# A hybrid pooling and gated-attention block on one core: the score recursion placed between the products of the projection pairs, and the pooling branch placed in front

## The chip, the cores and the metric

The kernel runs on one core of a Trainium2 chip. The metric is device time in microseconds for one execution of the whole block. The kernel before takes 1304.01 us, the median of three runs (1301.28 to 1304.34). The five engines of the core are written PE (matrix products), DVE (elementwise with two inputs), ACT (functions and copies), POOL (a second, slower elementwise engine) and SP (which issues the DMAs).

## The reference, cut to what matters

One encoder block on 1024 tokens of width 1024, with 16 meta tokens in front, in float32:

```python
z = u @ w_in;  a, q, k, v, r, lr, ga, gb = split(z)
p = multiscale_pool(a)                  # trailing means over 2, 4, 8, 16 tokens, minus the token
p = (p grouped @ w_pool_mix) * pool_scale;  y_a = p @ w_pool_out
log_a = log_sigmoid(lr @ w_gate_up + b_gate) / 16
# per chunk of 64 tokens and per head (4 heads, dk 64, dv 128):
b = cumsum(log_a);  scores = sum_k q_t k_s exp(-|b_t - b_s|)
o = scores @ v + (q exp(b)) @ S;  S = exp(b_end) S + (k exp(b_end - b))^T v
o = rmsnorm(o) * silu(r);  y_b = o @ w_gla_out
m = sigmoid(ga) * y_a + sigmoid(gb) * y_b
h = h + m @ w_out;  h = h + relu(rmsnorm(h) @ w_ff1)^2 @ w_ff2;  out = rmsnorm(h)
```

## The kernel before, in words

Every large product is made of three PE products of 128x128 weights with 512 columns (or 264): each float32 operand is split into a high part (rounded by ACT) and a low part (the difference, on DVE or POOL), and high x high, high x low and low x high are added (`mm3`). The order of the PE's work is the order in which the code is written. The other engines' instructions stand in an order that a scheduler makes from the dependences, and each engine then works its own queue in order.

The stages, in order of the program:

1. `start`: norm, transposition and the projections to v and to the low-rank decay input.
2. `proj_open` and `k_block`: differences of the transposed input for the next stage, and the projection to k (two blocks of 128 columns).
3. `pairs_of_projections`: the projections to q, r, gb and ga, eleven pairs of 128-column blocks. Each pair takes seven products (a Strassen scheme: P1 to P7) of 12 matmuls, 77 products in all. `sums_weights` makes the sums of weights that a product needs (four per pair, on DVE), and `split` parts them (ACT, then DVE), three products ahead, in four slots. After each product DVE combines sums of banks (`u2`, `u3`, `c`), and `put_...` finishes an output: for a gate ACT takes Abs, Exp and Ln, DVE one operation (`sigmoid`), ACT one more Exp, and a DMA stores it in HBM.
4. `gla`, the attention stage. The matmuls of `fill` run between the steps of the attention: the four blocks of `a_block` (the projection to the pooled columns), `mix_block` (pooling sums on DVE and 24 matmuls), the 16 blocks of `ya_block`, and the `yb_block`s of the first half of the tokens. A unit is a pair of heads p with a half of the tokens, four in all. `inside` computes the scores of a unit by a recursion of six levels: per level two multiplications on DVE (`grow`), a copy on ACT, 32 small matmuls (`scores`) and one predicated copy on DVE into `scc`. `across` then does what needs the state: transposition of k, eight chained state updates on DVE, the products with v and with the state, the norm, and the second transposition. Each unit's `inside` runs beside the `across` of the unit before it. `pour` drives the filling work by written costs: each step yields a cost, and as much filling work follows, times `PACE`.
5. The second half of `yb_block`, the output product (`out_tile`), and the two feed-forward products.

Buffers of the stages lie over one another: the left and right stacks are popped at each stage's opening. PSUM has eight banks; in the pairs stage four (`y`), two (`z`) and two (`sc`).

Of the kernel before, what the change touches and what calls it, by code (L numbers as in the profile page):

```python
# [31 lines left out]
PACE, LEVEL, OPENING = 1.0, 1.6, 10.0  # L32
# [71 lines left out]
def kernel(  # L104
# [34 lines left out]
    def two(tag):  # L139

        if tag == "sc":
            if "sc" not in wide:
                wide["sc"] = psp["sc"].tile([P, 2, 512], F32, name="b_sc", tag="sc")
            return wide["sc"]
        return psp[tag].tile([P, 2, 512], F32, name=f"b_{tag}", tag=tag)
# [7 lines left out]
    q_dram = dp.tile([2, 2, P, HALF], F32, name="q_dram")  # L153
    v_dram = dp.tile([2, 8, P, 2 * P], F32, name="v_dram")
# [6 lines left out]
    small = left.push("small", [P, 160], F32)  # L161
    small_at = [0]

    def tiny(n):
        a = small_at[0]
        small_at[0] += n
        assert small_at[0] <= 160
        return small[:, a : a + n]
# [6 lines left out]
    metab = left.push("metab", [P, 4, 16], F32)  # L175
    lrT_meta = left.push("lrT_meta", [16, 32], F32)[:, :META]
# [9 lines left out]
    MH, ML = [], []  # L186
# [185 lines left out]

    base = left.mark()
# [62 lines left out]
    def proj_open():  # L436

        left.pop_to(base)
        right.pop_to(1)
        S["t"] = [tuple(left.push(f"t{i}{k}", [P, 4, HALF], F32R) for k in "hl") for i in range(4)]  # L440
        buffer("t1", 2)
        buffer("o", 3)
        piece = lambda half, j: S["xr"][:, 4 * j : 4 * j + 4, half * HALF : (half + 1) * HALF]
        b11, b21, b12, b22 = (piece(h, j) for h in range(2) for j in range(2))

        def parts(i, a, eng=dve):
            hi, lo = S["t"][i]
            act.activation(hi, a, ACT.Copy)
            eng.tensor_tensor(lo, a, f32(hi), ALU.subtract)

        dve.tensor_tensor(b11, b12, b11, ALU.subtract)
        parts(0, b11)
        pool.tensor_tensor(b12, b22, b12, ALU.subtract)
        dve.tensor_tensor(b22, b22, b11, ALU.subtract)
        parts(1, b22)
        dve.tensor_tensor(b21, b21, b22, ALU.subtract)
        parts(2, b12, pool)
        parts(3, b21)

    step(one, proj_open)  # L460

    def k_block(p):
        def evac(b, half, at, n):
            o = nxt("o")[:, :n]
            act.activation(o, b, ACT.Copy)
            c = at if half == 0 else META + HALF
            nc.sync.dma_start(k_dram[p, :, c : c + n], o)

        return lambda wb: project(wb, WITH_META, evac)

    for p in range(2):
        step(one, k_block(p), W1, [w_cols(C_K + p * P)])
# [10 lines left out]
    def put_q(d, half, b):  # L483
        o = nxt("o")
# [3 lines left out]
    def put_r(h, half, b):  # L488
        t, o = sigmoid(b), nxt("o")
# [4 lines left out]
    def put_gate(dram):  # L494
        def put(d, half, b):
            t, o = sigmoid(b), nxt("o")
            act.activation(o, t, ACT.Exp)
            nc.sync.dma_start(dram[d, half], o)

        return put  # L500
# [48 lines left out]
    def sums_weights(n_pairs, load):  # L549

        for p, i in sums_order(n_pairs):
# [3 lines left out]
            else:  # L555
                a21, a22 = (w1raw[i, 1][:, k : k + 4] for k in (0, 4))
                s = quad(S["fs"][:, i % 2] if p != "P7" else S["s3"])
                if p == "P5":
                    dve.tensor_tensor(s, a21, a22, ALU.add)
                elif p == "P6":  # L560
                    dve.tensor_tensor(s, s, a11, ALU.subtract)
                elif p == "P7":
                    dve.tensor_tensor(s, a11, a21, ALU.subtract)
                elif p == "P3":
                    dve.tensor_tensor(s, a12, s, ALU.subtract)
# [11 lines left out]
    def pairs_of_projections():  # L577
# [10 lines left out]
        buffer("c", 3, HALF, right)  # L588
        load(1, 0)
        load(1, 1)  # L590
        banks(keep=1, y=4, z=2)
        w1_slots()
        plain = lambda half, j: tuple(t[half][:, 4 * j : 4 * j + 4, OFF[half] : OFF[half] + HALF] for t in (TH, TL))
        x = {"P1": plain(0, 0), "P2": plain(0, 1), "P5": S["t"][0], "P3": plain(1, 1)}
        x.update(zip(("P6", "P7", "P4"), S["t"][1:]))
        xb, zb = {}, {}
        left_over = 7 * len(PAIRS)
        W1.shift = 1
        for p, i, (ah, al) in ahead(sums_weights(len(PAIRS), load), 3):
# [9 lines left out]
            left_over -= 1  # L609
            if left_over == 2:  # L610
                raw.back()
                enqueue(rest)
                W1.top_up(1)
# [4 lines left out]
            elif p == "P2":  # L618
                put(d, 0, xb.pop(i))
            elif p == "P6":  # L620
                dve.tensor_tensor(u2, b, u2, ALU.add)
            elif p == "P7":
# [3 lines left out]
                put(d + 1, 1, c)  # L626
            elif p == "P4":
                c = nxt("c")
                dve.tensor_tensor(c, b, u3, ALU.add)
                put(d + 1, 0, c)  # L630
            elif p == "P3":
                c = nxt("c")
                dve.tensor_tensor(c, zb.pop(i), u2, ALU.add)
                put(d, 1, c)
            yield

# [3 lines left out]

    def told(name):
        step(fill, lambda: done.add(name))

    def gla_open():
        W1.eng = pool
        left.pop_to(base)
        right.pop_to(0)
        S["yg"] = {1: right.push("yg1", [P, 2, HEADS, HALF], F32R)}
        S["kq"] = [right.push(f"kq{h}", [P, 2, 2, HALF + OFF[h]], F32) for h in range(2)]
        S["v"] = right.push("v", [P, 2, 4, 2 * P], F32)  # L650
        for p in range(2):
            for h in range(2):
                c = slice(META + HALF, None) if h else slice(0, META + HALF)
                nc.sync.dma_start(S["kq"][h][:, p, 0], k_dram[p, :, c])
                nc.sync.dma_start(S["kq"][h][:, p, 1, OFF[h] :], q_dram[p, h])
        load_v(0)
        buffer("t1", 3, HALF, right)
        buffer("o", 3, HALF, right)
        push = right.push
        S["N"] = [push(f"n{i}", [P, HALF, 2], F32) for i in range(2)]  # L660
        S["F"] = push("f", [P, HALF, 2], F32)
        S["yt"] = push("yt", [P, 2, HALF], F32)
        S["ends"] = push("ends", [P, HALF], F32)
        S["scc"] = push("scc", [P, 2, 2, 4, CH], F32)
        S["S"] = push("S", [P, 2, 2, P], F32)
        S["W"] = push("W", [P, NC - 1, P], F32)

        mix = push("mix", [P, 4, HALF], F32)
        S["kt"], S["qe"], S["kl"], S["g"] = quad(mix[:, 0]), mix[:, 1], mix[:, 2], mix[:, 3]
        S["on"], S["sr"] = mix[:, 0:2].rearrange("p a (b c) -> p (a b) c", b=4), mix[:, 2:4]  # L670
        S["right_gla"] = right.mark()
        buffer("a", 4, 1056, right)
        banks(keep=1, mm=3, m2=1, ms=1)

    def load_v(half):
        for p in range(2):
            nc.sync.dma_start(S["v"][:, p], v_dram[p, 4 * half : 4 * half + 4].rearrange("t p c -> p t c"))

    step(rest, gla_open)

    pooled = {}

    def a_block(g):
        def fn(wb):
            a = pooled[g] = nxt("a")

            def evac(b, half, at, n):
                c = at if half == 0 else META + HALF
                act.activation(a[:, c : c + n], b, ACT.Copy)

            yield from project(wb, WITH_META, evac)

        return fn

    def pool_open():
        left.pop_to(left_ff)
        S["pm"] = left.push("pm", [P, 2, 4, SEQ], F32R)
        S["ph"] = left.push("ph", [P, 2, SEQ], F32R)
        buffer("s", 2, 1056)
        mw = S["mw"] = left.push("mw", [P, 2, 4, P], F32R)  # L700
# [113 lines left out]
    for g in range(4):  # L814
        step(fill, mix_block(g))
# [632 lines left out]
```

## Time and profile before

| | before |
|---|---|
| time, median of three | 1304.01 us |
| time of the profiled execution | 1304.01 us |
| its span, first to last instruction | 1302.2 us |
| granted PE clock, mean of the span | 0.975 |
| PE busy | 1225.4 us (94%) |
| DVE busy | 881.4 us (68%) |
| ACT busy | 635.2 us (49%) |
| POOL busy | 77.4 us (6%) |

The profiled execution's own time is 1.8 us more than its span, and it is the median of the runs. In the profile, L and a number is a line of the kernel; a row of a group gives the engine, the line, the written tile and the read tiles with their shapes, how often it ran, busy time and mean duration, and the idle time of the engine ahead of it with what ended that. A row of the timeline gives the start and the duration in us. A row of the stage table gives a stretch from A to B, its length, and the busy time of PE, its weight load, DVE, ACT and POOL in it, then the granted share of the PE clock, the DMA engines' share and GB/s.

### The profile page before, as it was taken

The page shows a single profiled execution, that of the slowest core. Times are in us where ns is not written, and L with a number is a line of the kernel's source. Part 1 is how long each engine was busy: PE and PEld are TensorE (multiplying, and loading weights), DVE is VectorE, ACT ScalarE, POOL GpSimd, SP SyncE. Part 2 cuts the span into 40 slices and gives each one's busy share as a digit, 9 for nine tenths or more (in the row PEclk, how much of TensorE's full clock was granted, in tenths as well). Part 3 has the DMA queues.
Part 4 walks back from the last instruction along what each step waited for, and adds up shares of the span by engine and source line. Part 5 has one row for each costly group of instructions (what it writes and reads, how often), then busy time and mean ns, then how long its engine had stood idle before and what let it go on. Part 6 is the DMA issues. An engine that isn't in the chain of part 4 may idle for free.

```text
span 1302.2 us, 18212 instructions
## 1 busy us (share of the span) xinstructions
PE 1225.4 (94%) x6763; PEld 1005.7 (77%) x6763; DVE 881.4 (68%) x1433; ACT 635.2 (49%) x1115; POOL 77.4 (6%) x42
## 2 busy tenths in 40 slices
PE   5999999999993989699999999999999999999997
PEld 4997888888772767588878888888887788888776
DVE  4563776676569668573588676767665777887686
ACT  6643576777443333231465455455454444444544
POOL 2120000000111013340000000000000000000000
PEclk9999999999995989799999999999999999999999
DMA  7322343423510456482125444354459873333532
GB/s 233 104 57 74 99 120 97 128 83 113 180 42 32 138 170 187 163 290 65 81 81 162 146 162 154 134 167 153 157 177 350 293 260 105 98 91 96 162 90 89
DMA packets 149721, 181.74 MB, mean 140 GB/s; under 512 B 11488, under 2 KB 88560, under 8 KB 149632
## 3 DMA queue, kind: packets, MB, share of 16 engines
q1 hardware_dynamic: 149632, 180.58, 43.1%
q8 instruction: 53, 0.87, 0.3%
q14 instruction: 36, 0.29, 0.1%
HBM read 123.90 MB, written 56.64 MB: 139 GB/s over the span
## 4 chain that ended last, share of the span: by engine, by line
PE 77%; DVE 8%; ACT 2%; issue 2%; DMA 2%; SPq 0%; POOL 0%; ACTq 0%; DVEq 0%; POOLq 0%
PE b_o L257 7%; PE b_o L258 7%; PE b_o L256 7%; PE b_y L256 6%; PE b_y L257 6%; PE b_y L258 6%; PE b_mm L256 5%; PE b_mm L257 5%; PE b_mm L258 5%; PE b_z L257 4%; PE b_z L258 4%; PE b_z L256 4%; PE b_sc L256 3%; PE b_sc L257 3%; PE b_sc L258 3%
## 5 line engine op out<-in xcount | busy, mean ns | idle before, releaser
L525 ACT ACTIVATE w1h<-raw 128x512 fp32r<-128x512 f32 x106 | 65.9, 623 | 54.4 <-PE b_y L257 17.3
L526 DVE TENSOR_TENSOR w1l<-raw,w1h 128x512 fp32r<-128x512 f32 x106 | 72.7, 686 | 23.8 <-ACT w1h L525 23.8
L525 ACT ACTIVATE w1h<-fs 128x512 fp32r<-128x512 f32 x81 | 51.2, 632 | 63.9 <-PE b_y L257 39.8
L256 PE MATMUL b_o<-w1h 128*128 128x512 f32 x192 | 75.4, 393 | 2.7 <-DVE h L1274 1.7
L257 PE MATMUL b_o<-w1l,w1h 128*128 128x512 f32 x192 | 74.9, 390 | 1.3 <-DVE w1l L526 1.3
L258 PE MATMUL b_o<-w1h,w1l 128*128 128x512 f32 x192 | 75.3, 392 | 0.1
L526 DVE TENSOR_TENSOR w1l<-fs,w1h 128x512 fp32r<-128x512 f32 x81 | 55.6, 687 | 24.7 <-ACT w1h L525 24.7
L76 POOL TENSOR_TENSOR w1l<-raw,w1h 128x1024 fp32r<-128x1024 f32 x14 | 35.1, 2508 | 405.0 <-ACT w1h L75 405.0
L1322 DVE TENSOR_TENSOR bt<-w,w 128x512 f32<-128x512 f32 x80 | 54.8, 685 | 3.1 <-DMA w<-in_w_ff_dram 3.1
L525 ACT ACTIVATE w1h<-bt 128x512 fp32r<-128x512 f32 x45 | 28.4, 632 | 58.1 <-issue 33.8
L257 PE MATMUL b_o<-fxl,fxh 128*128 128x512 f32 x128 | 50.3, 393 | 0.6 <-DVE small L215 0.6
L256 PE MATMUL b_sc<-mh,w1h 128*128 128x512 f32 x128 | 50.1, 392 | 0.8 <-ACT u2p L1246 0.8
L256 PE MATMUL b_mm<-wo,mh 128*128 128x512 f32 x128 | 50.7, 396 | 0.0
L257 PE MATMUL b_z<-ml,w1h 128*128 128x512 f32 x128 | 49.9, 390 | 0.4 <-DVE ml L1134 0.4
L258 PE MATMUL b_mm<-wo,ml 128*128 128x512 f32 x128 | 50.2, 392 | 0.0
L257 PE MATMUL b_mm<-wo,mh 128*128 128x512 f32 x128 | 50.2, 392 | 0.0
L258 PE MATMUL b_o<-fxh,fxl 128*128 128x512 f32 x128 | 50.2, 392 | 0.0
L257 PE MATMUL b_sc<-ml,w1h 128*128 128x512 f32 x128 | 50.0, 391 | 0.0
L256 PE MATMUL b_o<-fxh 128*128 128x512 f32 x128 | 49.9, 390 | 0.0
L258 PE MATMUL b_sc<-mh,w1l 128*128 128x512 f32 x128 | 49.8, 389 | 0.0
L258 PE MATMUL b_z<-mh,w1l 128*128 128x512 f32 x128 | 49.8, 389 | 0.0
L256 PE MATMUL b_z<-mh,w1h 128*128 128x512 f32 x128 | 49.8, 389 | 0.0
(353 smaller groups left out, 3663.6 us busy)
## 6 DMA issues: line engine op xcount, KB each, us to landing
hf_dram<-h SPq DMA_DIRECT2D x112, 256.0 KB, 2.0
raw<-hf_dram SPq DMA_DIRECT2D x112, 256.0 KB, 2.7
w<-in_w_ff_dram SPq DMA_DIRECT2D x64, 256.0 KB, 4.7
raw<-in_w_in_dram SPq DMA_DIRECT2D x22, 512.0 KB, 4.5
raw<-in_w_ff_dram SPq DMA_DIRECT2D x16, 512.0 KB, 4.2
rawx<-in_w_ff_dram SPq DMA_DIRECT2D x16, 512.0 KB, 4.3
rawp<-in_w_in_dram SPq DMA_DIRECT2D x10, 512.0 KB, 4.4
xs<-in_x_dram SPq DMA_DIRECT2D x8, 512.0 KB, 5.2
```

Of the source, the lines that this page charges most:

```text
L76: self.eng.tensor_tensor(lo, raw, hi.bitcast(F32), ALU.subtract)
L256: pe.matmul(ps, ah, bh, start=first and i == 0, stop=False, skip_group_check=more)
L257: pe.matmul(ps, ah, bl, start=False, stop=False, skip_group_check=more)
L258: pe.matmul(ps, al, bh, start=False, stop=last and i == n - 1, skip_group_check=more)
L525: act.activation(hi, a, ACT.Copy)
L526: dve.tensor_tensor(lo, a, f32(hi), ALU.subtract)
L1322: dve.tensor_tensor(bt, w, S["w2"][q[3:]][:, i], ALU.add if q[2] == "+" else ALU.subtract)
```

## The change

The change does six things.

- **The pooling branch moves in front.** `pool_open`, the four `a_block`s and the four `mix_block`s run after `start`, between and beside the k blocks: a0, a1, mix0, a2, mix1, a3, mix2, k0, mix3, the differences, k1. The mixed result goes to HBM (`pm_dram`), and is loaded and split again at the end of the pairs stage (`pooled_parts`: four loads, four ACT copies and four DVE subtractions of 1024 columns).
- **The score recursion moves into the pairs stage.** From the twelfth of the 77 products on, after each product steps of the chain `insides()` follow by written costs over `STRETCH` (1.9). It runs the four `inside` units one after the other, and the two `meta_state`s. A finished unit's scores and its two decayed factors go to HBM (`gi_dram`, 768 KB a unit) and the decays stay in a small tile. The scores have their own two PSUM banks (`gs`); the `y` banks fall from four to two.
- **The sums of weights of the pairs stage go from DVE to POOL** (`sums_weights(..., pool)`); the feed-forward stage keeps them on DVE.
- **The gates are stored ahead of their last Exp**; `ga_load` and `yb_load` take it on ACT after loading.
- **Only the state part stays in the attention stage.** `across` loads its unit's factors and scores; two units are live at a time, each with buffers of its own; `fill` holds `ya_block` and the first half of `yb_block`. `PACE` goes from 1.0 to 1.6 and `OPENING` from 10 to 6. v is loaded once, for both halves.
- **Merged and pooled operands lie over the transposed input** (`TH`, `TL`), and the last of the four differences is written over the input's own place after k1.

```diff
-PACE, LEVEL, OPENING = 1.0, 1.6, 10.0
+PACE, LEVEL, OPENING, STRETCH = 1.6, 1.6, 6.0, 1.9
...
+    for f, i in ((a_, 0), (a_, 1), (m_, 0), (a_, 2), (m_, 1), (a_, 3), (m_, 2), (k_, 0), (m_, 3)):
+        f(i)
+    step(one, differences)
+    k_(1)
+    step(one, lambda: S["last_difference"]())
...
     def put_gate(dram):
-        def put(d, half, b):
-            t, o = sigmoid(b), nxt("o")
-            act.activation(o, t, ACT.Exp)
-            nc.sync.dma_start(dram[d, half], o)
+        return lambda d, half, b, o: nc.sync.dma_start(dram[d, half], sigmoid(b))
...
                 if p == "P5":
-                    dve.tensor_tensor(s, a21, a22, ALU.add)
+                    eng.tensor_tensor(s, a21, a22, ALU.add)
...
-        banks(keep=1, y=4, z=2)
+        banks(keep=1, y=2, z=2, gs=1)
...
+        chain, credit = insides(), 0.0
+        for n, (p, i, (ah, al)) in enumerate(ahead(sums_weights(len(PAIRS), load, pool), 3)):
...
+            if n > 10:
+                credit += 12 * 512 / 2400 / STRETCH
+                while credit > 0 and chain:
+                    w = next(chain, None)
+                    if w is None:
+                        chain = None
+                    else:
+                        credit -= w
+            if total - n == 6:
+                pooled_parts()
...
+            b = scores(n[:, :, 0], n[:, :, 1])
+            dve.copy_predicated(scc, mask[:, lvl : lvl + 1, None, :].broadcast_to([P, 2, 4, CH]), b)
+            yield LEVEL
+        nc.sync.dma_start(gi_dram[p, half], gi)
...
+            act.activation(gates[n], gates[n], ACT.Exp)
...
-    for g in range(4):
-        step(fill, a_block(g), W1, [w_cols(C_A + g * P)])
-    step(fill, pool_open)
-    for g in range(4):
-        step(fill, mix_block(g))
...
+        waiting, live, since = [across(*u) for u in UNITS], [], 9
+        while waiting or live:
+            if waiting and len(live) < 2 and since > 1:
+                live.append(waiting.pop(0))
+                since = 0
+            since += 1
+            waits = [(g, next(g, None)) for g in live]
+            live = [g for g, w in waits if w is not None]
+            pour(max([w for _, w in waits if w is not None], default=0) * PACE)
```

On DVE in the middle of the pairs stage, this stood before: splits of weights (`w1l`), a sum of weights (`s`), and the combining and sigmoid steps (`c`, `t`, `o`).

```order
L629 TENSOR_TENSOR c<-b_y,u3p 128x512
L491 SCALAR_TENSOR_TENSOR o<-c,small,t_984 128x512
L526 TENSOR_TENSOR w1l<-raw_113,w1h 128x512
L480 SCALAR_TENSOR_TENSOR t_984<-c,t_984 128x512
L526 TENSOR_TENSOR w1l<-s_1181,w1h 128x512
L563 TENSOR_TENSOR s_1181<-raw_113,raw_117 128x512
```

The same engine in the same stage now, where `gi` is the tile of the scores, `n` and `f` the recursion's factors and `ends` its decays:

```order
L843 COPY_PREDICATED gi<-mask,b_gs 128x512
L814 TENSOR_TENSOR n_1614<-n_1618,ends 128x64x2x4
L816 TENSOR_TENSOR f<-n_1618,ends 128x64x8
L677 TENSOR_TENSOR u3p<-b_y,u2p 128x512
L584 TENSOR_TENSOR w1l<-fs,w1h 128x512
L679 TENSOR_TENSOR c<-b_z,u3p 128x512
L843 COPY_PREDICATED gi<-mask,b_gs 128x512
L814 TENSOR_TENSOR n_1618<-n_1614,ends 128x32x2x8
L816 TENSOR_TENSOR f<-n_1614,ends 128x32x16
L543 SCALAR_TENSOR_TENSOR t_962<-c,t_962 128x512
L584 TENSOR_TENSOR w1l<-fs,w1h 128x512
```

The sums of weights have left the queue, and a level's predicated copy and two multiplications stand ahead of a product's split and combining step.

On PE, the mixing matmuls (`ph,mw`) stood before in the attention stage, behind a level of the scores (`n`) and the last matmuls of an `a_block` (`th`, `tl`):

```order
L257 MATMUL b_mm<-tl_141,w1h 128x512
L258 MATMUL b_mm<-th_137,w1l 128x512
L880 MATMUL b_sc<-n_2774 64x64 x16
L256 MATMUL b_mm<-ph,mw 128x512
L257 MATMUL b_mm<-ph,mw 128x512
L258 MATMUL b_mm<-ph,mw 128x512
```

They now stand in front of the pairs stage, each group behind a whole further `a_block` or k block:

```order
L258 MATMUL b_mm<-th_139,w1h 128x512
L259 MATMUL b_mm<-tl_143,w1h 128x512
L260 MATMUL b_mm<-th_139,w1l 128x512
L258 MATMUL b_ms<-ph,mw 128x512
L259 MATMUL b_ms<-ph,mw 128x512
L260 MATMUL b_ms<-ph,mw 128x512
```

Nothing of the recursion stands between them any more.

On PE at the end of the attention stage, nine matmuls of the filling work (`yg_3842`, the last three shown) stand between the last unit's products with the state and its second transposition (`on`), and the second half's first matmuls (`yg_3838`) follow at once:

```order
L258 MATMUL b_mm<-yg_3842,w1h 128x512
L259 MATMUL b_mm<-yg_3842,w1h 128x512
L260 MATMUL b_mm<-yg_3842,w1l 128x512
L1024 MATMUL b_sc<-ident,on_3874 128x128 x8
L258 MATMUL b_mm<-yg_3838,w1h 128x512
L259 MATMUL b_mm<-yg_3838,w1h 128x512
```

The filling work has run out there; before, the last unit's transposition had no matmul at all between it and the products with the state.

540 lines of the change are left out of this document (266 added, 274 removed).

## The prediction

> **What bounds the kernel now.** I read the page first, for the share of each engine and the course over the span, then the stage table, then the waits of PE in the slowest stage.
>
> ```profile
> span 1302.2 us, 18212 instructions
> PE 1225.4 (94%) x6763; PEld 1005.7 (77%) x6763; DVE 881.4 (68%) x1433; ACT 635.2 (49%) x1115; POOL 77.4 (6%) x42
> PE   5999999999993989699999999999999999999997
> PEclk9999999999995989799999999999999999999999
> ```
>
> PE is the bound nearly everywhere, and the clock is full there. The exception is slices 13 to 17, some 390 to 550 us, where PE is not busy all the time and its clock falls. They lie in the attention stage. In the stage table the rows are the k blocks, the pairs stage, the attention stage, the first piece of the second half, and a piece of the attention stage by itself:
>
> ```profile
> 82.60:105.20 22.60, 22.60 (x147) 20.68 (x145) 11.97 (x8) 6.40 (x11) 4.01 (x1) 1.00 0.30 83
> 105.20:320.80 215.60, 212.62 (x927) 173.34 (x926) 141.46 (x216) 142.12 (x246) 0.00 (x0) 1.00 0.35 102
> 320.80:548.90 228.10, 185.24 (x1952) 146.98 (x1950) 156.51 (x267) 86.13 (x146) 42.64 (x21) 0.88 0.41 130
> 548.90:568.10 19.20, 18.10 (x74) 14.10 (x73) 16.54 (x16) 9.51 (x11) 6.91 (x4) 0.96 0.76 252
> 390.00:430.00 40.00, 18.34 (x72) 11.91 (x73) 33.88 (x41) 12.10 (x20) 4.31 (x2) 0.62 0.08 27
> ```
>
> The attention stage has 42.9 us without PE (228.1 - 185.2) and a granted clock of 0.88 besides. From 390 to 430 us, where the pooling sums run, PE is busy for 18.3 of 40 us at a clock of 0.62, and DVE for 33.9. The waits of PE in the stage say the same:
>
> ```profile
> PE b_mm L256 <- ACT ph L718: 21.0, 4, 6.5
> PE b_m L1006 <- DVE mix L1002: 8.5, 3, 5.2
> PE b_sc L880 <- DVE scc L941: 7.2, 3, 3.8
> ```
>
> 21.0 us are the mixing matmuls behind the pooling sums, 8.5 the second transposition behind the norm, 7.2 the scores behind the predicated copy.
>
> **What the stage would take without waits.** The pairs stage gives the price of a matmul of 512 columns, 212.6 us over 77 x 12 = 924, so 0.230 us. The k blocks give that of 264 columns: 22.6 us for 48 of 512 and 96 of 264, so 0.12. The small groups and a run of scores with the matmul behind it stand here:
>
> ```profile
> L978 PE MATMUL b_m<-v,scc 64*64 64x128 f32 x128 | 7.9, 272 | 1.6 <-DVE W L971 1.1 <-DVE S L971 0.5
> L1006 PE MATMUL b_m<-ident,mix 128*128 128x128 f32 x32 | 6.0, 349 | 8.5 <-DVE mix L1002 8.5
> L965 PE MATMUL b_m<-v,mix 64*64 64x128 f32 x128 | 4.4, 275 | 0.2 <-ACT mix L960 0.2
> L988 PE MATMUL b_m<-W,mix 64*64 64x128 f32 x112 | 4.4, 276 | 0.3 <-DVE small L983 0.3
> L959 PE MATMUL b_ms<-ident,mix 128*128 128x128 f32 x16 | 2.4, 275 | 0.9 <-DVE gB L857 0.9
> L827 PE MATMUL b_ms<-gB,wgu 16*128 16x512 f32 x8 | 4.5, 640 | 1.4 <-ACT metab L828 1.4
> 347.86 0.71 PE L880 MATMUL b_sc<-n 64*64 64x64 f32 x32
> 348.50 0.50 PE L256 MATMUL b_mm<-th,w1h 128*128 128x512 f32 x1
> ```
>
> Four pooled blocks at 11.3 us (half of the k stage) are 45; 24 mixing, 192 pooled-output and 96 gated-output matmuls at 0.230 are 72; 28 runs of scores at 0.64 (348.50 - 347.86) are 18; the decays 4.5, and some 2 for the meta state; the state part 7.9 + 6.0 + 4.4 + 4.4 + 2.4 = 25, which holds tails and slow clock, so between 20 and 27 with its rows that are left out. That is 162 to 169 us of 228.1: waits and slow clock cost 59 to 66. I take **62 us** to be won at most.
>
> **The change part by part.**
>
> *The pooling branch in front* takes its 51 us of matmuls along at full clock, and its DVE work to a place where DVE has room: it was busy for 12.0 of the 22.6 us of the k blocks.
>
> ```profile
> L715 DVE SCALAR_TENSOR_TENSOR s<-s,a 128x1024 f32<-128x1024 f32 x4 | 5.3, 1331 | 0.0
> L712 DVE TENSOR_TENSOR s<-s 128x1024 f32<-128x1024 f32 x3 | 3.6, 1215 | 0.0
> L449 DVE TENSOR_TENSOR t1l<-xr,t1h 128x2048 fp32r<-128x2048 f32 x1 | 5.8, 5795 | 3.7 <-PE b_ms L369 3.7
> ```
>
> The widest window needs four sums of 1.2 us, one of 1.33 and two splits, some 8 us, and the block in front of its matmuls lasts 11.3: hidden. If that cover were gone it would be the 21 us of before. The last difference can start only behind k1, and it stands in DVE's queue ahead of the splits of the third product, which PE reaches 5.5 us later: an ACT copy and a subtraction of 2048 columns, 4 to 6 us by the row of 5.8 us (which includes a block by POOL). Cost **2 us**, between 0 and 6.
>
> *The recursion in the pairs stage.* Of the 77 products, the written costs (4 x 16.1 + 2 x 6 = 76.4 over 2.56 / 1.9 a product) give it 57, from the 12th to the 68th. PE there: 57 x 12 x 0.230 = 157, plus 18 of scores and 7, so 182 us. DVE there:
>
> ```profile
> L526 DVE TENSOR_TENSOR w1l<-fs,w1h 128x512 fp32r<-128x512 f32 x33 | 22.7, 687 | 15.4 <-ACT w1h L525 15.4
> L480 DVE SCALAR_TENSOR_TENSOR t<-c,t 128x512 f32<-128x512 f32 x28 | 19.3, 688 | 9.9 <-ACT t L479 9.9
> L941 DVE COPY_PREDICATED scc<-mask,b_sc 128x512 f32<-128x512 uint8 x24 | 17.6, 734 | 4.8 <-PE b_sc L880 4.8
> L912 DVE TENSOR_TENSOR f<-n,ends 128x512 f32<-128x512 f32 x16 | 11.0, 684 | 0.0
> L899 DVE TENSOR_TENSOR n<-kq,mix 128x512 f32<-128x512 f32 x4 | 3.3, 826 | 3.1 <-ACT mix L892 3.0
> ```
>
> 57 splits, 40 combining steps, 32 sigmoid steps and 7 of r at 0.69 to 0.75 are 94 us; 24 predicated copies 17.6, 40 multiplications of levels at 0.684 27, eight first ones 6.6, decays, last halves and meta state some 15: 66. Together 160 of 182 us, 88%. So DVE would just keep up by itself. But the sums go to POOL, and POOL and DVE get in each other's way:
>
> ```profile
> 351.78 2.39 POOL L76 TENSOR_TENSOR w1l<-raw,w1h 128x1024 fp32r<-128x1024 f32 x1 [15.90 <-ACT w1h L75]
> 352.20 2.52 DVE L910 TENSOR_TENSOR n<-n,ends 128x512 f32<-128x512 f32 x1
> 354.64 0.68 DVE L912 TENSOR_TENSOR f<-n,ends 128x512 f32<-128x512 f32 x1
> 392.06 2.26 POOL L703 TENSOR_TENSOR mw<-raw,mw 128x512 fp32r<-128x512 f32 x1
> 393.10 0.72 DVE L941 COPY_PREDICATED scc<-mask,b_sc 128x512 f32<-128x512 uint8 x1
> L807 POOL TENSOR_TENSOR ml<-t,mh 128x512 fp32r<-128x512 f32 x8 | 10.2, 1276 | 15.5 <-ACT mh L806 15.5
> ```
>
> A multiplication with both operands in SBUF, of 0.68 us, takes 2.52 when POOL has begun a little before it: it ends where POOL does. A predicated copy that reads PSUM runs beside POOL in its usual 0.72. By the list above about 102 of the 160 us on DVE have both operands in SBUF (39 of splits, 41 of levels, decays and last halves, 22 of sigmoid and r steps). A sum on POOL takes 1.28 us by the row of the same size; 33 of the 44 lie in the stretch. At 64% a block of 1.28, less what DVE can do first, I price each at 0.8 us: 26 us. DVE then needs 186 of 182 us. [...]
>
> A queue that is worked in order also waits: before, DVE waited 15.4 us for ACT ahead of 33 splits, 0.47 each. When DVE is the bound, such waits reach PE. Lower end 0 (POOL costs nothing, 160 of 182); upper end 33 x 1.28 + 57 x 0.47 + 160 - 182 = 47. The splits run three products ahead, some 8 us of cover, which is used up once. I take **12 us**, near the low end, since 186 is nearly 182.
>
> Such waits would be short and should leave the clock alone: over the first products of the pairs stage PE was busy for 8.0 of 11 us in pieces, and the clock was full.
>
> ```profile
> 107.00:118.00 11.00, 8.02 (x32) 5.58 (x31) 3.81 (x6) 3.35 (x6) 0.00 (x0) 1.00 0.12 48
> ```
>
> *What is left of the attention stage.* 288 matmuls of 512 and the state part, some 90 us. The chain of a unit (transposition, eight updates, products, norm, transposition) now has 45 matmuls, 10 us, between its steps, except at the end, where nine are left, 2.1 us. Before it was this:
>
> ```profile
> 541.35 0.71 PE L988 MATMUL b_m<-W,mix 64*64 64x128 f32 x17
> 547.23 1.97 PE L1006 MATMUL b_m<-ident,mix 128*128 128x128 f32 x8 [5.17 <-DVE mix L1002]
> 548.85 0.77 PE L256 MATMUL b_mm<-yg,w1h 128*128 128x512 f32 x1
> ```
>
> 5.2 us less 2.1 is 3 us ahead of the transposition; behind it the second half needs the product, copy and difference of 1024 columns, where before there was filling work with other operands: about 3 us. At the start, the gates' loads stand in SP's queue behind the last gate's store, and three `mm` banks cover 8 us of it: 1 to 3 us. With the exponentials now on ACT in this stage (86 of 228 us busy, so room) I take **10 us**, between 6 and 30; the upper end is the 21 + 8.5 us of waits of before, as if as much were uncovered again.
>
> *The rest* costs nothing: `pooled_parts` needs four copies and four subtractions of 1.2 us behind the last read of the input's first half, with five products, 14 us, still to come; if they did not cover it, 5 to 10 us of the attention stage's opening.
>
> Sum: 62 - 2 - 12 - 10 = 38. Span 1302.2 - 38 = 1264.2; with the 1.8 us around it **1266 us**, against a median of 1304.01 that equals this execution.
>
> **The rivals.**
>
> *DVE keeps up* (0.17): the blocks fall into DVE's own waits, 34% of its time in the pairs stage before. The stage loses 1 us, the rest 9: 62 - 10 = 52, 1252 us. For it: 160 of 182. Against: the order has a level's steps in front of splits.
>
> *The attention stage waits on its loads* (0.13): the units' factors, v, the gates and the weights all come in there, and the neighbouring stretch already moved 252 GB/s at a DMA share of 0.76. Waits of 30 in place of 10: 1286 us.
>
> *Blocks cost their whole length* (0.10): 30 to 47 us in the pairs stage, 1284 to 1301.
>
> *DVE becomes the bound with a poor fill* (0.07), the case on the other side. In the attention stage DVE, working on this same recursion, was busy for only 156.5 of 228.1 us, 69%, since each level waits for PE and ACT. Over the whole pairs stage DVE has 201 us of work (160, and 41 for the other 20 products and the pooled parts) and 26 of blocks, and PE 237. At 74% busy it would last 307, 70 us more than PE: 62 - 70 - 12 = -20, 1324 us. It turns slower below 79% (50 us). Against: in the pairs stage it is not one chain; splits and combining steps fill its gaps.
>
> **How the numbers follow.** The forecast has 0.53: 1266. Differences under 0.3% (4 us) are no change here. Only the last rival is slower; with the edge of the fourth that makes faster 0.90, same 0.03, slower 0.07. The range reaches up over the loads' case and half of the fourth, to 1292, and down past the second's 1252 to 1246; what lies outside is the slow case, part of the fourth, and a full 62.
>
> **What would show it.** Right: the stretch from the k blocks' end to the attention stage lasts 250 to 265 us, with PE waiting for the scores' factors, splits or predicated copies and DVE over 85% busy; 24 mixing matmuls without waits; an attention stage of some 100 us to the second half, at a clock above 0.93, with its longest waits at its end. DVE operations of 0.68 us stand at up to 1.9 us beside POOL's sums. Wrong: a pairs stage of 240 (the blocks cost nothing) or over 285 us (DVE at a poor fill), or waits for DMA inside the attention stage.

## The result and the profile after

The changed kernel takes 1287.57 us (median of 4 runs, 1287.43 to 1288.13) against 1303.67 us (4 runs, 1301.28 to 1304.34): a ratio of 0.9881, 95% interval 0.9863 to 0.9898. It is 16 us faster; 38 were forecast. Among the runs of the experiments below three executions are set apart by their length (1524.7, 1762.1 and 6526.8 us; the first ran at a granted clock of 0.75) and enter no comparison. The page of the profiled execution after, span and shares, then PE's busy tenths and its granted clock in 40 slices:

```profile
span 1286.3 us, 18286 instructions
PE 1225.8 (95%) x6763; PEld 1000.7 (78%) x6763; DVE 855.2 (66%) x1389; ACT 637.0 (50%) x1119; POOL 125.4 (10%) x82
PE   5999989999998898799999999999999999999997
PEclk8999999999999899899999999999999999999999
```

The hole of before, in slices 13 to 17 with a clock down to 5 tenths, has become three slices in which PE is busy for 7 or 8 tenths (the 14th, 16th and 17th), and two of them, the 14th and the 17th, have a clock of 8. (The 6th slice, at the opening of the pairs stage, has 8 tenths too.) The stage table gives the stages: the front (k blocks and now the pooling branch), the pairs stage to its last `b_z` matmul, the attention stage to the last transposition, and the rest. After the length come PE busy, PEld, DVE, ACT, POOL, then clock, DMA share and GB/s.

```profile
84.50:157.90 73.40, 73.40 (x458) 66.64 (x457) 33.11 (x31) 29.72 (x45) 4.60 (x1) 1.00 0.27 80
157.90:416.50 258.60, 247.88 (x1843) 190.91 (x1842) 193.69 (x314) 166.47 (x291) 60.19 (x44) 0.99 0.41 126
416.50:531.60 115.10, 97.11 (x722) 76.87 (x722) 61.90 (x104) 41.77 (x65) 30.93 (x16) 0.92 0.65 216
531.60:1286.30 754.70, 738.40 (x3233) 600.14 (x3231) 527.58 (x864) 353.24 (x622) 12.69 (x8) 1.00 0.47 156
```

| stage | before | forecast | after | after less forecast |
|---|---|---|---|---|
| start | 82.6 | 82.6 | 84.5 | +1.9 |
| front | 22.6 | 75.6 (51 and 2 more) | 73.4 | -2.2 |
| pairs | 215.6 | 252.6 (25 of work, 12 of waits more) | 258.6 | +6.0 |
| attention | 228.1 | 100 (90 of work, 10 of waits) | 115.1 | +15.1 |
| rest | 753.3 | 753.3 | 754.7 | +1.4 |

The last column sums to 22 us, which is the distance between 38 and 16. Most of it is the attention stage, where PE is idle for 115.1 - 97.1 = 18.0 us. Its waits of over 1 us there:

```profile
PE b_sc L1024 <- DVE on L1020: 7.3, 1, 7.3
PE b_mm L258 <- DVE o L911: 4.8, 1, 4.8
PE b_mm L258 <- DVE t L950: 3.7, 1, 3.7
```

Each happens once. The clock follows them. The stretches that the records show at half clock, cut out as windows (two in the pairs stage, three in the attention stage):

```profile
253.00:256.40 3.40, 3.40 (x10) 2.63 (x9) 0.90 (x2) 2.33 (x5) 1.15 (x1) 0.50 0.28 18
307.60:311.00 3.40, 3.40 (x8) 2.67 (x9) 0.68 (x1) 2.58 (x4) 0.00 (x0) 0.50 0.20 77
430.50:437.30 6.80, 6.18 (x41) 4.57 (x42) 3.04 (x7) 2.39 (x4) 0.00 (x0) 0.50 0.82 265
509.00:515.80 6.80, 6.22 (x23) 4.44 (x23) 5.15 (x6) 2.21 (x3) 5.51 (x4) 0.50 0.56 183
526.10:532.90 6.80, 3.24 (x12) 2.95 (x13) 4.60 (x9) 2.44 (x4) 2.21 (x2) 0.50 0.50 167
```

In the second stretch wide matmuls start 0.43 us apart (308.02 to 310.58), behind it 0.23. In the last three PE worked for 6.2 + 6.2 + 3.2 = 15.6 us, so by estimate they cost up to half of that, some 7.8 us, and the first two up to 3.4. With 18.0 of waits and 7 to 8 of half clock on 90 of work, the stage's 115.1 us are accounted for. This holds for the profiled execution; the other three of the same kernel ran at a mean granted clock of 0.981 to 0.982 in place of its 0.986 and were 0.5 to 0.7 us shorter, so there nearly the same time is split in another way between waits and half clock; how is not known. Each of the attention stage's three stretches of 6.8 us comes with one of the waits of 3.7 to 7.3: in the 3.4 us ahead of it (427.1 to 430.5, 505.6 to 509.0, 522.7 to 526.1) PE was busy for 0.00, 0.28 and 0.00 us.

What is behind the waits stands in the other engines' timelines (start, duration, engine, line, operation, then in brackets the idle time before it and its releaser; SPq is the queue from which SP issues the DMAs):

```profile
421.42 3.17 SPq L889 DMA_DIRECT2D t<-ga_dram  x3
429.72 1.95 ACT L890 ACTIVATE t<-t 128x512 f32<-128x512 f32 x3 [4.18 <-DMA t<-ga_dram]
430.38 2.01 DVE L911 TENSOR_TENSOR o<-b_mm,t 128x512 f32<-128x512 f32 x3 [9.88 <-ACT t L890]
501.08 0.63 ACT L926 ACTIVATE t<-t 128x512 f32<-128x512 f32 x1 [3.63 <-DMA t<-gb_dram]
502.14 1.00 ACT L1016 ACTIVATE on<-b_m 128x1024 f32<-128x1024 f32 x1
503.18 1.22 DVE L1018 TENSOR_REDUCE small<-on 128x8 f32<-128x1024 f32 x1 [6.82 <-ACT on L1016]
507.89 0.68 DVE L950 TENSOR_TENSOR t<-b_mm,t 128x512 f32<-128x512 f32 x1
```

At the opening, the first gate loads are issued at 421.4, behind two units' factors and v; ACT waits for them until 429.7, DVE cannot empty the `mm` banks before 430.4, and PE has used up its three banks. At 501 the same happens one step removed: ACT waits 3.6 us for a gate load, the norm's square (L1016) stands behind that in ACT's queue, the norm is late on DVE, and the emptying of a bank (L950) stands behind the norm. PE's wait is put down to DVE; a DMA began it.

### The profile page after: what moved, and what is told of

It is laid out like the page before. It is cut to its first block, busy times and chain, and to the rows that moved or that the text cites. A ratio compares the mean times of both kernels' runs of the same rounds, so it can differ in the third digit from the quotient of the medians.

```text
span 1286.3 us, 18286 instructions
## 1 busy us (share of the span) xinstructions
PE 1225.8 (95%) x6763; PEld 1000.7 (78%) x6763; DVE 855.2 (66%) x1389; ACT 637.0 (50%) x1119; POOL 125.4 (10%) x82
## 4 chain that ended last, share of the span: by engine, by line
PE 75%; DVE 9%; DMA 7%; ACT 4%; issue 3%; POOL 1%; SPq 1%; DVEq 0%; ACTq 0%
PE b_mm L258 7%; PE b_o L259 7%; PE b_o L260 7%; PE b_mm L259 7%; PE b_o L258 7%; PE b_mm L260 7%; PE b_y L258 5%; PE b_y L260 4%; PE b_y L259 4%; PE b_z L258 3%; PE b_z L259 3%; PE b_z L260 3%; PE b_sc L258 3%; PE b_sc L259 3%; PE b_sc L260 3%
## 5 line engine op out<-in xcount | busy, mean ns | idle before, releaser
L258 PE MATMUL b_sc<-th,w1h 128*128 128x512 f32 x216 | 86.5, 400 | 5.6 <-ACT u2p L671 2.6
L258 PE MATMUL b_z<-th,w1h 128*128 128x512 f32 x216 | 86.3, 399 | 1.2 <-DVE c L679 0.8
L259 PE MATMUL b_z<-tl,w1h 128*128 128x512 f32 x216 | 85.1, 394 | 0.4 <-DVE tl L1148 0.4
L259 PE MATMUL b_sc<-tl,w1h 128*128 128x512 f32 x216 | 84.7, 392 | 0.0
L260 PE MATMUL b_z<-th,w1l 128*128 128x512 f32 x216 | 84.6, 392 | 0.0
L260 PE MATMUL b_sc<-th,w1l 128*128 128x512 f32 x216 | 84.5, 391 | 0.0
L258 PE MATMUL b_mm<-th,w1h 128*128 128x512 f32 (+1 forms) x208 | 72.9, 350 | 5.7 <-DVE o L911 4.8
L259 PE MATMUL b_mm<-tl,w1h 128*128 128x512 f32 (+1 forms) x208 | 71.8, 345 | 0.0
L260 PE MATMUL b_mm<-th,w1l 128*128 128x512 f32 (+1 forms) x208 | 71.7, 345 | 0.0
L258 PE MATMUL b_mm<-wo,th 128*128 128x512 f32 x128 | 50.7, 396 | 0.0
```

Of the source, the lines that this page charges most:

```text
L258: pe.matmul(ps, ah, bh, start=first and i == 0, stop=False, skip_group_check=more)
L259: pe.matmul(ps, ah, bl, start=False, stop=False, skip_group_check=more)
L260: pe.matmul(ps, al, bh, start=False, stop=last and i == n - 1, skip_group_check=more)
```

## The experiments

Theory A: what was lost lies in these three waits and the half clock behind them, two of them begun by gate loads, and in the recursion's own work in the pairs stage. Its rivals: POOL's sums hold up DVE (B), the waits come from order or buffers and not from loads (C), the earlier units need all of their filling work (D). Differences in us are to the changed kernel's 1287.57; each ratio is to the kernel before, run along with it (1302.7 to 1303.7 us).

### Sums of weights back on DVE

```diff
-        for n, (p, i, (ah, al)) in enumerate(ahead(sums_weights(len(PAIRS), load, pool), 3)):
+        for n, (p, i, (ah, al)) in enumerate(ahead(sums_weights(len(PAIRS), load, dve), 3)):
```

> The sums of the weights' blocks go back from POOL to DVE; everything else as in the changed kernel. Theory A (the missing time lies in the attention stage's waits and the half clock after them, and in the recursion's own work on TensorE): DVE was busy for 193 of the 257.6 us of the pairs stage, 44 sums of about 0.7 us more make it some 220, still under TensorE, so the time stays within 4 us of 1287.6. Rival B (the sums on POOL hold up DVE, as the prediction priced with 26 us of blocks): without POOL's work the pairs stage loses most of its 10.7 us of waits, 1278 to 1283.

Measured: 1281.8 us, ratio to before 0.9841 (0.9826 to 0.9856), 5.8 faster (3.3 between the two kernels further down that differ in this alone at a lower pace). The pairs stage:

```profile
155.40:409.50 254.10, 246.21 (x1843) 189.52 (x1841) 204.57 (x359) 166.47 (x291) 0.00 (x0) 0.99 0.42 128
```

PE's waits there are 7.9 in place of 10.7 us. DVE's work rose by only 11 us, although 44 sums of 0.69, 30 us, came to it: the other 19 were time that DVE had lost beside POOL (the recursion's 16 multiplications `n`, for one, took 0.95 us on the mean beside POOL's sums and 0.68 without). The time lies in B's range and outside A's, but B's mechanism is only part of it. The stage fell by 4.5 us; 2.8 of them are waits, where B had most of the 10.7 going, and 1.7 are PE's busy time, by estimate the one stretch at half clock that this execution has less (one of 3.4 us, at 301.6, for two). POOL's sums did cost something, 3 to 6 us, but DVE was not the bound either way (194 busy of 258.6 us, 205 of 254.1).

### No gate loads

```diff
-            nc.sync.dma_start(gates[n], ga_dram[n // 2, n % 2])
-            act.activation(gates[n], gates[n], ACT.Exp)
+            act.activation(gates[n], gB[:, :HALF], ACT.Exp)
...
-            nc.sync.dma_start(gl, gb_dram[d, h])
             nc.sync.dma_start(ml, ma_dram[d, h])
-            act.activation(gl, gl, ACT.Exp)
+            act.activation(gl, gB[:, :HALF], ACT.Exp)
```

> The gates of both branches are not loaded from DRAM: the exponential reads a tile that stands in SBUF instead, so 8 MB of loads are left out and the output is not the reference's. Theory A with loads as the cause of its first two waits (TensorE's wait of 4.8 us at the stage's opening and of 3.7 us in its second half trace back to gate loads that ScalarE waits for): both go, and with each about 3.4 us of half clock; attention stage from 116 to 98 to 104 us, time 1271 to 1277. Rival C (the waits come from DVE's order or from free buffers, the load was only the last to arrive): they stay in another place, 1283 to 1288.

Measured: 1270.5 us, 17 faster (0.9752, 0.9725 to 0.9779). The pairs stage, the attention stage, and the latter's only wait of over 1 us (the edits shift line numbers by a few):

```profile
157.90:413.40 255.50, 244.89 (x1844) 188.60 (x1842) 194.59 (x315) 166.39 (x291) 59.80 (x44) 1.00 0.41 125
413.40:513.20 99.80, 90.33 (x721) 73.22 (x722) 59.40 (x104) 44.02 (x68) 31.02 (x16) 0.96 0.58 191
PE b_sc L1022 <- DVE on L1018: 8.3, 1, 8.3
```

Both of the waits traced to gate loads are gone with their half clock: the stage fell by 15.3 us, and C falls. The time is half a us below A's range. The last unit's wait is still there, at 8.3 us for 7.3, so it has another cause. A side reading: in this execution the pairs stage, which the edit does not touch, had a full clock, and was 3.1 us shorter. PE's busy time there fell by 3.0, which is what its two stretches at half clock cost.

### Less filling work given out ahead

```diff
-PACE, LEVEL, OPENING, STRETCH = 1.6, 1.6, 6.0, 1.9
+PACE, LEVEL, OPENING, STRETCH = 1.35, 1.6, 6.0, 1.9
```

> PACE 1.35 instead of 1.6: less of the filling work is given out ahead, so about 39 of the 288 filling products and not 9 are left for the last unit's chain of normalisation. Theory A: the wait of 7.3 us at the end shrinks under 2 us and the 6.8 us at half clock behind it go; 8 to 10 us faster, 1278 to 1281. Rival D (the chains of the earlier units need all of their filling work): waits of the same sum appear ahead of the earlier units, 1285 to 1290.

Measured: 1274.0 us, 13.5 faster (0.9790, 0.9764 to 0.9816). Attention stage, rest, and the stage's two longest waits:

```profile
414.00:511.50 97.50, 90.37 (x713) 72.72 (x713) 54.75 (x100) 38.47 (x59) 21.50 (x12) 0.96 0.71 233
511.50:1272.40 760.90, 741.87 (x3241) 602.29 (x3239) 534.43 (x869) 357.26 (x628) 20.61 (x13) 0.99 0.48 158
PE b_mm L258 <- DVE o L911: 4.4, 1, 4.4
PE b_sc L1024 <- DVE on L1020: 1.3, 1, 1.3
```

The last wait fell from 7.3 to 1.3. The rest grew by 6.2 us, since nine of the filling matmuls now run behind the stage's end, the second half's opening waits more, and a stretch of 3.4 us at half clock (519.6) falls into it; the stage itself fell by 17.6. More went than A had said: the wait in the middle is gone too, presumably since PE, with fewer matmuls ahead of each step, no longer uses up its banks before the gate is there; this was not tried apart. D falls at this pace.

### The recursion left out of the pairs stage, and its scores twice

```diff
-        chain, credit = insides(), 0.0
+        chain, credit = None, 0.0
```

(with zeros stored for the scores, factors, decays and states), and in another kernel

```diff
-                pe.matmul(b[to, e, j], kk[r, s], qq[r, s], ...)
+                for _ in range(2):
+                    pe.matmul(b[to, e, j], kk[r, s], qq[r, s], ...)
```

> The recursion and the meta state are left out of the pairs stage (zeros are stored in place of their results, so the output is not the reference's); the sums stay on POOL. Theory A: the recursion costs this stage its own work on TensorE (some 34 us by the busy time), two stretches at half clock and the waits, so the stage returns to 215 to 220 us: 1246 to 1252. Rival B (the sums on POOL cost the stage time by themselves): the stage stays above 225 us, 1256 or more.

> Every matmul of the scores is issued twice (64 in place of 32 for each of 28 runs). This parts the small matmuls' own work from what a change between 512 wide and 64 wide matmuls costs. If the changes cost 0.3 to 0.4 us a run, as the intervals in the trace show, the added 896 matmuls cost only 16 ns each, 14 us: 1300 to 1304. If a run's whole 1.2 us is the work of its 32 matmuls, they cost 34 us: 1317 to 1324.

Measured: 1243.6 us without the recursion, 44 faster (0.9548, 0.9534 to 0.9563); with the scores twice a ratio to before of 1.0011 (0.9997 to 1.0026), some 17 us above the changed kernel. The two pairs stages:

```profile
156.40:374.00 217.60, 212.93 (x925) 172.97 (x924) 130.35 (x181) 131.98 (x221) 57.37 (x44) 1.00 0.40 120
157.20:431.10 273.90, 264.14 (x2739) 207.48 (x2738) 194.00 (x315) 167.99 (x291) 59.24 (x44) 0.99 0.39 119
```

Without the recursion the stage takes 217.6 us even with POOL's sums, as A had it (the whole kernel is 2 us under A's range). Before it took 215.6, so the sums alone cost at most 2 us; the rest of what they cost comes only beside the recursion. Against the 244.9 us busy of the same stage at full clock (the kernel without gate loads), the recursion's work on PE is 244.9 - 212.9 = 32.0 us, where the prediction had 25. The second set of scores added 264.1 - 247.9 = 16.3 us of PE busy, 18 with the half clock taken out (one stretch of 3.4 us here, two there), for 896 matmuls: 20 ns each, 0.64 a run. That is nearer to the 14 us of the first case than to the 34 of the second, but above it. So the work of the scores is 28 x 0.64 = 18, as priced. The timeline of the changed kernel shows what came on top:

```profile
204.41 0.39 PE L260 MATMUL b_y<-t2h,w1l 128*128 128x512 f32 x1
204.72 0.70 PE L775 MATMUL b_gs<-gi 64*64 64x64 f32 x32
205.35 0.50 PE L258 MATMUL b_sc<-th,w1h 128*128 128x512 f32 x1
205.69 0.39 PE L259 MATMUL b_sc<-tl,w1h 128*128 128x512 f32 x1
```

From start to start it is 0.31 into the run and 0.34 behind the first wide matmul after it, where two wide ones stand 0.23 apart: 0.08 and 0.11 us for the two changes of shape, by estimate 5 us for 28 runs like this one. That leaves 9 of the 32.0 for the decays and the meta state, priced at 7; this is a difference and was not measured by itself.

### Gates loaded earlier

```diff
-        buffer("t1", 3)
+        buffer("t1", 4)
...
             fetch(p, 0)
+            for _ in range(2):
+                ga_load()
...
-                    while len(gates) < min(2 * d + h + 2, 16):
+                    while len(gates) < min(2 * d + h + 3, 16):
```

> One more buffer for the gates and the sigmoids (4 in place of 3), so gates are loaded one step further ahead, and the first four gate loads are issued right behind the first unit's factors, ahead of v. Theory A with loads as cause: the wait of 4.8 us at the opening falls under 1.5 us and the one of 3.7 us at the second half of the stage goes, each with its half clock; without gate loads the stage was 99.8 us, here 100 to 105, time 1272 to 1277. If the DMA engines simply can't bring all that is due in these 15 us, v comes later in exchange, and the first unit's state products wait for it: 1282 to 1288.

> The four gate buffers and the early gate loads alone, once more, for a profile at full clock (the first profile of this kernel fell to a granted clock of 0.75 throughout). Theory A: 1277 to 1281 again; the opening's wait of 4.8 us and its half clock are gone, and since the time fell by 8 us and not by the 17 of the kernel without gate loads, the wait in the middle of the stage, which ScalarE's wait for a gate load starts, is still there with 2 to 4 us, and the last unit's wait with 7 to 8.

Measured: runs of 1274.5 to 1280.2 us the first time, 0.9806 (0.9780 to 0.9832), and 1278.6 the second, 0.9804 (0.9777 to 0.9830): 8 to 9 faster. The attention stage and its waits, from the second:

```profile
414.50:522.40 107.90, 93.45 (x721) 74.34 (x722) 62.86 (x104) 41.61 (x65) 30.44 (x16) 0.94 0.69 231
PE b_sc L1026 <- DVE on L1022: 7.1, 1, 7.1
PE b_mm L258 <- DVE t L952: 4.5, 1, 4.5
PE b_mm L258 <- DVE o L913: 0.7, 1, 0.7
```

The opening's wait fell from 4.8 to 0.7, and the stage by 7 us. The first expectation was wrong about the middle, and its 1272 to 1277 us are for most runs too low. The second, made with this time in hand, was nearly right: the middle's wait stays, at 4.5 for 2 to 4. Since another order of the loads and one more buffer removed the opening's wait, the DMA engines could bring all that was due (231 GB/s over the stage, at a DMA share of 0.69).

### Useless matmuls in the last wait

```diff
+        if (p, half) == (1, 1):
+            warm = bank("ms")
+            for _ in range(30):
+                pe.matmul(warm, S["yg"][0][:, 0, 0, :P], S["yg"][0][:, 0, 0], start=True, stop=True)
```

> 30 matmuls whose result nobody reads (6.9 us at full clock) are put ahead of the last unit's transposes, in the place where TensorE waits for 7.3 us; nothing else changes. If the half clock behind that wait costs time of its own, as the records show (6.8 us at half), it goes and the time falls by 3 to 4 us, to 1283.5 to 1284.5, though TensorE does more work. If only the wait costs, the time stays at 1287 to 1288 or rises a little.

Measured: 1290.0 us (0.9896, 0.9877 to 0.9915), 2.4 slower, within the intervals. It tells nothing about the clock: ACT's queue came out in another order, with work for the second half ahead of the last unit's copy (`yg`, L1031). PE's waits, then ACT:

```profile
PE b_mm L258 <- ACT yg L1031: 6.0, 1, 6.0
PE b_sc L1028 <- DVE on L1020: 1.3, 1, 1.3
532.15 1.06 ACT L1092 ACTIVATE wo<-raw 128x1024 fp32r<-128x1024 f32 x1 [0.61 <-DMA raw<-in_w_out_dram]
533.12 1.04 ACT L1031 ACTIVATE yg<-sr 128x1024 fp32r<-128x1024 f32 x1
```

The wait was covered and came back behind the transposition, 6.0 us long, with 10.2 us at half clock after it.

### The edits together, and the meta state's steps apart

All four (sums on DVE, PACE 1.35, gates early with four buffers) are one kernel; the next leaves the gates as they were; another has all four with PACE 1.2.

> The four edits at once: sums on DVE, PACE 1.35, four gate buffers, first gate loads ahead of v. Theory A: the gains measured alone were 6 (sums on DVE) and 13.5 (PACE), and the opening's wait with its half clock is 7 to 8 more; the wait in the middle is gone with PACE already. 1260 to 1265. If the edits shift the same waits about, 1270 to 1275.

> PACE 1.35 and the sums on DVE, without the early gates: what the gates add to the kernel with all four edits. Theory A: the opening's wait of 4.4 us and its half clock of 6.8 us come back, so 5 to 8 us slower than all four edits: 1272 to 1275. If the early gates only move the wait elsewhere once the pace is lower: 1266 to 1269.

> All four edits with PACE 1.2. The last unit's wait is 1.3 us already, so little is left to win there; the earlier units lose 3 to 6 more filling products each. Theory A: the earlier units' chains begin to show as waits, 1267 to 1272. Rival: the rest of the waits at the end and at the opening of the second half, 4.0 us, goes too, 1261 to 1265.

Measured: 1267.2 us with all four (0.9721, 0.9702 to 0.9740), between the two expectations, so the gains do not add up in full; 1270.7 without the early gates (0.9751, 0.9732 to 0.9770), 1267.2 at PACE 1.2 (0.9723, 0.9707 to 0.9740), in A's range: nothing more is won. Without the early gates the opening's wait is back; their worth here, 3.5 us, lies between the two expectations, and the intervals overlap. At PACE 1.2 a unit's chain shows as a wait; the longest wait in the attention stage without the early gates:

```profile
PE b_mm L258 <- DVE o L911: 4.7, 1, 4.7
```

and at PACE 1.2, where it is the wait for a unit's updates of the state (`w`):

```profile
PE b_m L1002 <- DVE w L995: 4.7, 1, 4.7
```

The last kernel adds to the four edits:

```diff
-PACE, LEVEL, OPENING, STRETCH = 1.35, 1.6, 6.0, 1.9
+PACE, LEVEL, OPENING, STRETCH = 1.35, 1.6, 6.0, 1.7
...
-        yield 1.0
+        yield 3.0
...
         dve.tensor_copy(S["S"][:, 0, p], b[:, :P])
+        yield 2.0
```

> All four edits, and the meta state's steps stand further apart in the pairs stage (3.0 in place of 1.0 after the transposed factors' copy, 2.0 more behind the state's copy; STRETCH 1.7 so that the recursion still ends in time). Theory A: TensorE's four waits there, 2.4 us in all, and the stretch of 6.8 us at half clock that follows two of them go: 3 to 6 us faster than with the four edits, 1261 to 1264. If the half clock has nothing to do with these waits, it appears again at about the same place: 1265 to 1268.

Measured: 1264.5 us, 0.9697 (0.9676 to 0.9719), 2.8 less than the four edits, between the two expectations; the intervals overlap, so the stages say more than the time. The pairs stage with the four edits, then this kernel's pairs and attention stages:

```profile
156.30:412.00 255.70, 247.79 (x1843) 190.40 (x1841) 204.64 (x358) 166.62 (x291) 0.00 (x0) 0.99 0.42 127
157.50:407.60 250.10, 244.59 (x1843) 188.48 (x1841) 204.63 (x359) 165.23 (x291) 0.00 (x0) 1.00 0.42 129
407.60:500.80 93.20, 87.57 (x712) 70.75 (x713) 56.44 (x100) 38.81 (x60) 21.36 (x12) 1.00 0.75 248
```

The pairs stage fell by 5.6 us: the meta state's waits (2.4 us with the four edits) are gone, and so are the 6.8 us at half clock that stood at 301.6; the clock is full through both stages. Of the kernels that compute the whole block it is the fastest, 23 us under the changed one and 39 under before; the forecast had been 38, for another kernel.

## Why the prediction was wrong in size

The direction was right, and the time lies in the forecast's range of 1246 to 1292 us; the gain was 16 us where 38 were forecast. Step by step:

- **62 us at most**: nothing speaks against it. The last kernel won 39 with 7 us more of work in the recursion than priced.
- **The pooling branch in front, 2 us**: it cost next to nothing. PE was busy for 73.4 of 73.4 us, so the mixing matmuls had no waits, and over the first products of the pairs stage PE waited 3.4 us, where it had waited 3.0 before.
- **The recursion's work in the pairs stage, 25 us**: 32.0. The scores' 18 were right; the changes of shape (5) were left out, and decays and meta state (9 for 7) were under-priced. Some 3 us of half clock behind the meta state's waits came on top; the prediction held that short waits leave the clock alone. With 7.7 us more of waits this makes the 43 us by which the stage grew.
- **POOL's blocks and DVE, 12 us**: the wrong model, and a size that came near by luck. DVE was to be over 85% busy and was busy for 193.7 of 258.6 us, 75%; DVE was slowed beside POOL, by some 19 us, but had the room. More waits than before were 10.7 - 3.0 = 7.7 us, and 2.8 of them went with POOL's sums. One row was also misread: the multiplication of 2.52 us does not end where POOL does (351.78 + 2.39 = 354.17) but at 354.72, 0.55 us later, so by this row the block is POOL's remainder ahead of most of DVE's own 0.68.
- **What is left of the attention stage, "I take 10 us, between 6 and 30"**: this is the step that failed, as a term of the sum that was mis-sized. It was 25 (115.1 less 90): 18.0 of waits and some 7 of half clock. The end was priced at 3 us ahead of the transposition and took 7.3, since some 2 us of filling work cover a chain that now lasts 9.6 us from the last product with the state to the transposition, where it lasted 5.2 before: the filling work's own steps stand between the norm's (rows below). The opening was priced at 1 to 3 us and took 4.8. The wait in the middle (3.7) had no term. And no wait in this stage had a price for the clock, though the trace of before showed 0.62 in such a place.
- **The rival with loads, 1286 us**: its mechanism is the cause of two of the three waits. That its time came within 2 us is partly luck: it put 20 us more on the loads than the forecast had, the kernel without gate loads won 17 us, 15 of them in the attention stage, and the pairs stage was 6 us longer than either had it. "Waits for DMA inside the attention stage" was named as what would make the forecast wrong. The other rivals fell: DVE had room, as the first of them had it, but the stage still lost 43 us and not 26; POOL's sums cost 3 to 6 us and not 30 or more; and DVE never became the bound.
- **Start and rest**: 1.9 and 1.4 us longer. Before has a stretch of 3.4 us at half clock near 24 us, the changed kernel one of 6.8, by estimate up to 1.7 of the 1.9. The other kernels, whose start is the same, show one or the other too; why was not looked into further.

What stays open: what the half clock behind the last unit's wait is worth by itself, since the useless matmuls moved other work; and the whole of why 8 to 9 us of early gates alone became 3.5 behind a lower pace. Part of it is in the traces: with all four edits PE waits 2.5 us for a unit's updates of the state, with 3.4 us at half clock behind it, and without the early gates 0.8.

ACT, DVE and POOL in the last unit's norm, in the changed kernel:

```profile
522.13 0.63 ACT L954 ACTIVATE th<-t 128x512 fp32r<-128x512 f32 x1 [2.62 <-DVE t L951]
522.67 1.01 ACT L1016 ACTIVATE on<-b_sc 128x1024 f32<-128x1024 f32 x1
524.84 0.68 DVE L950 TENSOR_TENSOR t<-b_mm,t 128x512 f32<-128x512 f32 x1
524.69 2.35 POOL L76 TENSOR_TENSOR w1l<-raw,w1h 128x1024 fp32r<-128x1024 f32 x1 [0.58 <-ACT w1h L75]
525.44 1.63 DVE L210 TENSOR_SCALAR small<-small 128x8 f32<-128x8 f32 x1
526.98 0.68 DVE L951 TENSOR_TENSOR t<-t,o 128x512 f32<-128x512 f32 x1
528.38 1.23 DVE L1020 TENSOR_TENSOR on<-b_sc,small 128x1024 f32<-128x1024 f32 x1
```

The square (L1016) and the scaling (L1020) are the chain; L954, L950 and L951 belong to the filling work, and L210, a step of 8 columns of the norm that took 0.17 us in the unit before, stood at 1.63: it ended at 527.07, where POOL's split of weights for the filling work did (524.69 + 2.35 = 527.04). By this row a block beside POOL, which the prediction priced in the pairs stage alone, is some 1.5 us of the last unit's chain.

## What to carry to other kernels

Where work is moved out of a stage, price what is left by its longest chain less the filling work that is really still there at that point, and add something for half clock where the trace shows it behind a wait (here, behind waits of 4.8, 3.7 and 7.3 us, by estimate up to 3.1, 3.1 and 1.6 us, half of PE's busy time in each stretch). Follow a load into the queue of the engine that consumes it: here an Exp that waited for a gate held up a norm, and the wait appeared at an engine and a line that have nothing to do with DMA. A pace that spends all filling work early leaves the last chain bare; one constant was worth 13.5 us.

## What was not expected of the hardware

Half clock (0.50 from 253.0 to 256.4 us and from 307.6 to 311.0) also came where PE's longest waits were 1.1 and 1.3 us. In the two windows of 3.4 us ahead of the pairs stage's half clock, PE was busy for 2.32 and for 1.58 us:

```profile
249.60:253.00 3.40, 2.32 (x8) 1.35 (x9) 2.32 (x5) 3.08 (x6) 1.79 (x2) 1.00 0.00 0
304.20:307.60 3.40, 1.58 (x8) 0.58 (x7) 2.56 (x5) 2.51 (x5) 1.27 (x1) 1.00 0.77 264
160.80:164.20 3.40, 1.74 (x8) 1.36 (x8) 1.08 (x1) 1.12 (x2) 2.78 (x3) 1.00 0.89 216
```

In the second, the decays and the meta state, all of them matmuls with 16 rows, are nearly all of it (0.43 + 1.12 of 1.58 us). PE's busy time alone does not tell where half clock follows: in the third window, at the opening of the same stage, PE was busy for 1.74 us, less than in the first, all of it wide matmuls, and the clock stayed full behind it (1.00 from 164.2 to 167.6 us). Whether the matmuls with 16 rows made the difference was not tried. Five profiled executions have the same recursion and POOL's sums in the pairs stage (the changed kernel and the edits to gate loads, PACE, early gates and useless matmuls); two of them have two such stretches and three have none. The meta state's waits are alike with and without (1.3, and 1.5 to 1.6 us for two, in the changed kernel, without gate loads, at PACE 1.35 and with early gates), and the stage is some 3 us shorter without (255.5 us without gate loads and 256.1 at PACE 1.35, both at a clock of 1.00, for 258.6 at 0.99). With the sums on DVE all four kernels that keep the meta state's steps close together have one stretch there (with all four edits 6.8 us, from 301.6 to 308.4, at 0.50), and the one in which these waits are gone has none (1.00 over the stage).
